# Four plain tiles instead of five in a gated channel mixer, and its block sums split 512 columns at a time

## The chip, the core and the metric

The kernel runs on one core of one Trainium2 chip. The metric is device time in microseconds (us): the median of several executions, beside one more execution that was profiled. A core has engines that work side by side, each through its own list of instructions in a fixed order: PE (TensorE, matmuls), DVE (VectorE), ACT (ScalarE), POOL (GpSimd), and SP, which here issues most DMAs. An engine's instruction waits until the instructions of other engines that it needs are done, and everything behind it on its engine waits with it.

## The reference

The reference is a two-layer trunk over 512 tokens of width 1024. Each layer has a token mixer (mLSTM in the first, banded attention in the second, with attention to a memory beside it) and then a channel mixer. The change is in the channel mixer alone:

```python
D_MODEL, SEQ = 1024, 512
D_FF = ((8 * D_MODEL // 3 + 127) // 128) * 128      # 2816

def causal_dwconv(x, w, b):
    k = w.shape[0]
    s = x.shape[1]
    xp = jnp.pad(x, ((0, 0), (k - 1, 0), (0, 0)))
    y = xp[:, 0:s] * w[0]
    for j in range(1, k):
        y = y + xp[:, j:j + s] * w[j]
    return y + b

def conv_ffn(h, w_up, conv_w, conv_b, w_down):
    u, g = jnp.split(h @ w_up, 2, axis=-1)
    g = causal_dwconv(g, conv_w, conv_b)
    return (jax.nn.silu(g) * u) @ w_down

# in each layer l
x = x + conv_ffn(rmsnorm(x, norm_ffn_g[l]), ffn_w_up[l], ffn_conv_w[l], ffn_conv_b[l], ffn_w_down[l])
```

## The kernel before

Everything is float32, and the kernel keeps its accuracy by splitting every operand of a matmul into a high part (`hi`, a cast on ACT, L140) and a low part (`lo`, the source minus `hi`, on DVE, L141). A product is then three matmuls: hi by hi, hi by lo, lo by hi (`mm3`, L194, L195, L196). Activations lie transposed, features on the 128 partitions and the 512 tokens along the columns. They are kept as pairs of tiles `u`.

The hidden width of a channel mixer is 2816, so it has 22 tiles of 128 hidden features, each with a gate and an up half. A tile is made in one of two ways.

- A **plain** tile (`plain`) multiplies gate and up in full: 8 blocks of the inner dimension, 512 columns, three matmuls each, for gate (into a `pmm` buffer of PSUM) and for up (`psc`). The weights of each half come by one DMA of 512 KB into a staging tile `wr`, of which there are three, and are split into `wh` and `wl`, of which there are three each. Behind the gate half come the three taps of the convolution (L692 on ACT, L685 twice on DVE), the silu (L722), the product with the up half (L727) and the split of the result (`keep`), which becomes `hid[j]`. The first three tiles also carry the factor of the norm (L718, L724).
- A **step** (`step`, from `later`) makes gate and up of one tile together with Winograd's form of Strassen's scheme: seven products of half the inner dimension and 256 columns, instead of eight. It needs sums of weight blocks (L888 on DVE, and their splits into `wh`, `wl`, `fh`, `fl`), and sums of activation blocks, which are made once per mixer.

The sums of activation blocks and the scaled activations come from the generator `forms`. It first yields eight times for the scaled tiles (L733) and their splits, then four times for the block sums: four subtractions of 256 columns (L751) and the splits of the results into parts, each time. `weave` takes a given share of a filler's yields per yield of a plain tile, so that `forms` runs between the blocks of plain tiles 1 to `PLAIN - 1`.

The down-projection is cut into 32 **units**, each 4 hidden tiles by 128 output features, 12 matmuls of 512 columns into one of two `ptr` buffers of PSUM (`down_products`). A unit's result is copied by ACT (L777) and added to DRAM by a DMA from POOL (L778). A pair of units shares one DMA of 512 KB and one split. `UNITS` says which units stand at which tile.

Two things set the order. Outside of `later` a scheduler orders each engine's list, so it may move instructions across the borders of the code's blocks. Inside `later` the lists of PE, ACT and DVE are written out by hand; the preparation of the first step stands ahead of that, and the scheduler may still place it between work of the last plain tile and its units.

Of the kernel before, what the change touches and what calls it, by code (L numbers as in the profile page):

```python
# [10 lines left out]
F32R = mybir.dt.float32r  # L11
# [5 lines left out]
P = 128  # L17
D = 1024
S = 512
# [20 lines left out]

PLAIN, UNSCALED, GROUP, LAST = 5, 3, 4, 6
UNITS = {PLAIN - 1: (0, 1, 2, 3), 5: (None, 4), 6: (None, 5), 7: (None, 6), 8: (None, 7)}
UNITS.update((j, (2 * j - 10, 2 * j - 9)) for j in range(9, 21))

H = S // 2
# [7 lines left out]
def trunk(  # L55
# [34 lines left out]
    def sb(tag, shape, dtype=F32):  # L90
        count[0] += 1
        return pool.tile(shape, dtype, tag=tag, name=f"{tag}{count[0]}", bufs=bufs[tag])

    def ps(tag):
        count[0] += 1
        return psum.tile([P, S], F32, tag=tag, name=f"p{tag}{count[0]}", bufs=pbufs[tag])
# [61 lines left out]
    turn = [0]  # L158
# [506 lines left out]
    class ChannelMixer:  # L665
# [64 lines left out]
        def forms(self):  # L730

            for j in range(KT):
                V.scalar_tensor_tensor(  # L733
                    xT[j], xT[j], self.gain[:, j : j + 1], self.norm.row, op0=ALU.mult, op1=ALU.mult
                )
                hi, lo = sb("u", [P, S], F32R), sb("u", [P, S], F32R)
                split(hi, lo, xT[j])
                self.ready.append((hi, lo))
                yield
            self.sums = []  # L740
            for k in range(KT // 2):
                b1, b2 = xT[k], xT[k + KT // 2]
                forms = []
                ta, tb = sb("t", [P, S]), sb("t", [P, S])
                for o, x, y in (
                    (ta[:, :H], b1[:, H:], b1[:, :H]),
                    (ta[:, H:], b2[:, H:], ta[:, :H]),
                    (tb[:, :H], b2[:, H:], b1[:, H:]),
                    (tb[:, H:], b2[:, :H], ta[:, H:]),
                ):  # L750
                    V.tensor_tensor(out=o, in0=x, in1=y, op=ALU.subtract)  # L751
                for t in (ta, tb):
                    for h in (t[:, :H], t[:, H:]):
                        both = sb("u", [P, S], F32R)
                        split(both[:, :H], both[:, H:], h)
                        forms.append(both)
                self.sums.append(forms)
                yield

# [3 lines left out]
            g, jj = divmod(q, KT // 2)  # L763
            return load(rows(ffn_w_down[self.l], 2 * jj * P, 2 * P, GROUP * g, GROUP * (g + 1)), GROUP, 2 * P)

        def down_products(self, u):
            g, j = divmod(u, KT)
            w = self.down[u // 2]
            o = ps("tr")
            c = slice(u % 2 * P, (u % 2 + 1) * P)  # L770
            for k in range(GROUP):
                mm3(o, w[0][:, k, c], w[1][:, k, c], *self.hid[GROUP * g + k], k == 0, k == GROUP - 1)
            return j, o

# [25 lines left out]

        def t(self, i):

            return [(p[i - 1][:, :H], p[i - 1][:, H:]) for p in self.sums]

        def later(self):

# [151 lines left out]
    def channel_mixer(l, act, norm, gain, beside):  # L958

        mixer = ChannelMixer(l, act, norm, gain, beside)  # L960
        forms = mixer.forms()
        run(mixer.plain(0))
        skips = -(turn[0] + 1) % 3
        for j in range(1, UNSCALED):
            turn[0] += j <= skips
            weave(mixer.plain(j), forms, KT / (16.0 * (UNSCALED - 1)))
# [2 lines left out]
        for j in range(UNSCALED, PLAIN):  # L969
            units = UNITS.get(j, ())  # L970
            raws = {u // 2: mixer.load_down(u // 2) for u in units[::2]}
            weave(mixer.plain(j), forms, 4 / (16.0 * (PLAIN - UNSCALED)))
            for u in units:
                if u // 2 not in mixer.down:
                    mixer.down[u // 2] = parts(raws[u // 2])
                mixer.add(*mixer.down_products(u))
        run(forms)
        mixer.later()
        reload_x()
# [303 lines left out]
    for j in range(KT):  # L1283
        wh, wl = weights(rows(ffn_w_down[0], j * P, P, FT - LAST, FT), LAST, P)
        o = ps("mm")
# [252 lines left out]
```

## Time and profile before

| | us |
|---|---|
| median of 3 executions | 1180.86 (1180.71 to 1181.27) |
| the profiled execution | 1181.04 |
| its span, first to last instruction | 1179.3 |
| PE busy | 1169.1 (99%) |
| DVE busy | 935.7 (79%) |
| ACT busy | 725.8 (62%) |
| POOL busy | 129.9 (11%) |

How the views are read: a row of the timeline is its start, its duration, engine, line, operation, output and input by the program's names, the size, and in brackets how long the engine was idle before and what ended that. Two matmuls that follow each other overlap, so the distance of their starts tells what one costs. Rows of the stretches give the stretch, then for each engine its busy time and number of instructions, the granted clock of PE, the DMA engines' busy share and GB/s. DMA rows give the size of a transfer and the median time from issue to landing.

The first mixer's plain tiles run from about 275 us of the span to 341, its steps to about 590; the second mixer's lie some 554 us later.

### The profile page before, as it was taken

Reading aid. Unit: us, or ns where it says so; the run is one execution under the profiler, and the core shown is the slowest. Engines: PE = TensorE matmul, PEld = TensorE weight load, DVE = VectorE, ACT = ScalarE, POOL = GpSimd, SP = SyncE. Lnnn points to the kernel's source line nnn. Section 1 sums busy time; section 2 is a strip of 40 time slices with the busy share of each in tenths; the row PEclk is TensorE's granted clock in tenths of the full one; section 3 lists DMA queues with packets and bytes.
Section 4 is the critical chain, followed back from the end, with each engine's and each line's share of the span. In section 5 each row is a group of like instructions: output and inputs, shape, how many; then the busy total and the mean of one; then the engine's idle time right before and its main releaser. Section 6 shows DMA issues by size and latency. Waiting matters only on the chain.

```text
span 1179.3 us, 18676 instructions
## 1 busy us (share of the span) xinstructions
PE 1169.1 (99%) x7007; PEld 1034.2 (88%) x7007; DVE 935.7 (79%) x1688; ACT 725.8 (62%) x1294; POOL 129.9 (11%) x222
## 2 busy tenths in 40 slices
PE   9999999999999999999999999999999999999997
PEld 9988888888889999999888888888889999999986
DVE  6877788887978877777698888897897877777755
ACT  6548677654655655555666667776565655555545
POOL 1111101000021111111020000101001011111100
PEclk9999999999999999999999999999999999999999
DMA  8645325244266677765564312335426466666551
GB/s 299 208 109 134 94 55 152 76 139 121 90 166 163 164 164 162 164 148 129 150 200 125 90 54 85 106 102 177 139 90 153 108 143 144 143 143 141 123 158 72
DMA packets 200156, 158.64 MB, mean 135 GB/s; under 512 B 8344, under 2 KB 179838, under 8 KB 200066
## 3 DMA queue, kind: packets, MB, share of 16 engines
q1 hardware_dynamic: 183906, 119.74, 34.6%
q0 software_dynamic: 15584, 36.67, 16.4%
q8 instruction: 55, 0.90, 0.3%
q10 hardware_dynamic: 576, 1.05, 0.2%
q14 instruction: 35, 0.29, 0.1%
HBM read 128.89 MB, written 32.46 MB: 137 GB/s over the span
## 4 chain that ended last, share of the span: by engine, by line
PE 94%; DVE 3%; ACT 1%; issue 0%; DMA 0%; SPq 0%; POOL 0%; ACTq 0%; POOLq 0%; DVEq 0%
PE pmm L194 18%; PE pmm L195 18%; PE pmm L196 18%; PE ptr L195 6%; PE ptr L194 6%; PE ptr L196 6%; PE psc L195 5%; PE psc L196 5%; PE psc L194 5%; PE psc L544 2%; PE ptr L1365 1%; PE ptr L1386 1%; PE ptr L1387 1%; PE ptr L627 1%; PE ptr L613 0%; DVE pt L141 0%
## 5 line engine op out<-in xcount | busy, mean ns | idle before, releaser
L194 PE MATMUL pmm<-u,wh 128*128 128x512 f32 (+1 forms) x968 | 333.2, 345 | 0.4 <-ACT u L140 0.2
L196 PE MATMUL pmm<-u,wl 128*128 128x512 f32 (+1 forms) x968 | 330.8, 342 | 0.0
L195 PE MATMUL pmm<-u,wh 128*128 128x512 f32 (+1 forms) x968 | 330.5, 342 | 0.0
L141 DVE TENSOR_TENSOR wl<-wr,wh 128x1024 fp32r<-128x1024 f32 (+3 forms) x172 | 199.6, 1162 | 101.8 <-ACT wh L140 101.4
L140 ACT CAST wh<-wr 128x1024 fp32r<-128x1024 f32 (+3 forms) x172 | 172.0, 1002 | 92.7 <-PE pmm L195 39.0
L196 PEld LDWEIGHTS pmm<-u,wl 128*128 128x128 f32 x968 | 181.9, 188 | 20.6
L194 PEld LDWEIGHTS pmm<-u,wh 128*128 128x128 f32 x968 | 181.8, 188 | 19.3 <-ACT u L140 1.1
L195 PEld LDWEIGHTS pmm<-u,wh 128*128 128x128 f32 x968 | 182.0, 188 | 18.5 <-DVE u L141 0.5
L194 PE MATMUL ptr<-u,wh 128*128 128x512 f32 x272 | 106.7, 392 | 0.0
L195 PE MATMUL ptr<-u,wh 128*128 128x512 f32 x272 | 106.5, 392 | 0.0
L196 PE MATMUL ptr<-u,wl 128*128 128x512 f32 x272 | 105.8, 389 | 0.0
L778 POOL DMA_DIRECT2D xspill<-t x64 | 55.6, 869 | 447.3 <-ACT t L777 437.5
L141 DVE TENSOR_TENSOR fl<-pt,fh 128x512 fp32r<-128x512 f32 x102 | 70.3, 689 | 11.2 <-ACT fh L140 8.5
L194 PE MATMUL pmm<-u,fh 128*128 128x256 f32 x272 | 75.4, 277 | 0.0
L195 PE MATMUL pmm<-u,fh 128*128 128x256 f32 x272 | 75.2, 276 | 0.0
L196 PE MATMUL pmm<-u,fl 128*128 128x256 f32 x272 | 75.2, 276 | 0.0
L195 PE MATMUL psc<-u,wh 128*128 128x256 f32 (+1 forms) x232 | 75.1, 324 | 0.0
L196 PE MATMUL psc<-u,wl 128*128 128x256 f32 (+1 forms) x232 | 75.1, 324 | 0.0
L194 PE MATMUL psc<-u,wh 128*128 128x256 f32 (+1 forms) x232 | 75.0, 324 | 0.0
L140 ACT CAST fh<-pt 128x512 fp32r<-128x512 f32 x102 | 62.7, 615 | 13.5 <-DVE pt L888 13.3
L950 ACT ACTIVATE t<-t 128x512 f32<-128x512 f32 x34 | 21.5, 632 | 79.2 <-DVE t L685 79.2
L777 ACT COPY t<-ptr 128x512 f32<-128x512 f32 x64 | 37.6, 587 | 51.6 <-PE ptr L196 51.6
(335 smaller groups left out, 2540.3 us busy)
## 6 DMA issues: line engine op xcount, KB each, us to landing
wr<-in_ffn_w_up_dram SPq DMA_DIRECT2D x54, 512.0 KB, 5.0
wr<-in_ffn_w_down_dram SPq DMA_DIRECT2D x38, 512.0 KB, 4.1
pt<-in_ffn_w_up_dram SPq DMA_DIRECT2D x34, 512.0 KB, 6.9
xspill<-t POOLq DMA_DIRECT2D x64, 256.0 KB, 4.7
wr<-in_a_w_in_dram SPq DMA_DIRECT2D x20, 512.0 KB, 3.8
wr<-in_w_kv_dram SPq DMA_DIRECT2D x12, 512.0 KB, 4.0
xspill<-fh POOLq DMA_DIRECT2D x16, 256.0 KB, 2.6
xspill<-fl POOLq DMA_DIRECT2D x16, 256.0 KB, 3.0
```

The lines of the kernel that those rows point to most:

```text
L140: high = A.copy(hi, src) if on_act else V.tensor_copy(hi, src)
L141: low = V.tensor_tensor(out=lo, in0=src, in1=f(hi), op=ALU.subtract)
L194: nc.tensor.matmul(o, lh, rh, start=first, stop=False, skip_group_check=more)
L195: nc.tensor.matmul(o, lh, rl, start=False, stop=False, skip_group_check=more)
L196: nc.tensor.matmul(o, ll, rh, start=False, stop=last, skip_group_check=more)
L544: nc.tensor.matmul(o, a, b, start=first and i == 0, stop=i == 1)
L627: nc.tensor.matmul(o2, vs[a][:, 2 * hp + h, :], p[h][:, a, :], start=i == 0, stop=i == 3)
L777: A.copy(t, o)
L778: G.dma_start(xspill[j], t, accum_op=ALU.add)
L950: A.activation(self.acc, self.acc, AF.Silu)
L1365: nc.tensor.transpose(tp[:, b * P : (b + 1) * P], es[T, h][:, b * P : (b + 1) * P], ident)
L1386: nc.tensor.matmul(o2[:, s * P :], w, hi_at(pts[h], s, s, TT - s), start=s == 0, stop=False)
```

## The change

`PLAIN` goes from 5 to 4: tile 4 becomes a step, so there are 18 steps instead of 17 in each mixer. Units 0, 1 and 2 stand behind the last plain tile, now tile 3, instead of units 0 to 3; unit 3 moves into the first step, tile 4. Since the units behind tile 3 need tile 3's own result, units 0 and 1 are started over their first three hidden tiles, and finished with the fourth (`k0`, `k1`, `o` of `down_products`). The four yields of the block sums now fall into one plain tile instead of two. Their parts are split as two pairs of 512 columns per pair of sums, instead of four of 256; the tiles `u` are as many as before. `skips` shifts by one which of the three weight buffers the tiles use. The number in brackets of `weave` changes with `PLAIN` by itself.

```diff
-PLAIN, UNSCALED, GROUP, LAST = 5, 3, 4, 6
-UNITS = {PLAIN - 1: (0, 1, 2, 3), 5: (None, 4), 6: (None, 5), 7: (None, 6), 8: (None, 7)}
+PLAIN, UNSCALED, GROUP, LAST = 4, 3, 4, 6
+UNITS = {PLAIN - 1: (0, 1, 2), 4: (None, 3), 5: (None, 4), 6: (None, 5), 7: (None, 6), 8: (None, 7)}
 UNITS.update((j, (2 * j - 10, 2 * j - 9)) for j in range(9, 21))
...
                 for t in (ta, tb):
-                    for h in (t[:, :H], t[:, H:]):
-                        both = sb("u", [P, S], F32R)
-                        split(both[:, :H], both[:, H:], h)
-                        forms.append(both)
+                    hi, lo = sb("u", [P, S], F32R), sb("u", [P, S], F32R)
+                    split(hi, lo, t)
+                    forms += [(hi[:, c], lo[:, c]) for c in (slice(0, H), slice(H, S))]
                 self.sums.append(forms)
                 yield
...
-        def down_products(self, u):
+        def down_products(self, u, k0=0, k1=GROUP, o=None):
             g, j = divmod(u, KT)
             w = self.down[u // 2]
-            o = ps("tr")
+            o = o or ps("tr")
             c = slice(u % 2 * P, (u % 2 + 1) * P)
-            for k in range(GROUP):
+            for k in range(k0, k1):
                 mm3(o, w[0][:, k, c], w[1][:, k, c], *self.hid[GROUP * g + k], k == 0, k == GROUP - 1)
             return j, o
...
         def t(self, i):
 
-            return [(p[i - 1][:, :H], p[i - 1][:, H:]) for p in self.sums]
+            return [p[i - 1] for p in self.sums]
...
         run(mixer.plain(0))
-        skips = -(turn[0] + 1) % 3
+        skips = -(turn[0] + 2) % 3
...
             weave(mixer.plain(j), forms, 4 / (16.0 * (PLAIN - UNSCALED)))
+            started = {}
             for u in units:
                 if u // 2 not in mixer.down:
                     mixer.down[u // 2] = parts(raws[u // 2])
-                mixer.add(*mixer.down_products(u))
+                if u < 2:
+                    started[u] = mixer.down_products(u, 0, GROUP - 1)[1]
+                if u == 1:
+                    for v, o in started.items():
+                        mixer.add(*mixer.down_products(v, GROUP - 1, GROUP, o))
+                if u >= 2:
+                    mixer.add(*mixer.down_products(u))
         run(forms)
         mixer.later()
```

The scheduler answers with another order at three places of each mixer; those of the first mixer are shown.

SP's list from tile 2's up weights on, before. `ffn_w_up` is gate, up or step weights, `ffn_w_down` the two loads for units 0 to 3.

```order
L153 DMA wr_3190<-in_ffn_w_up_dram 128x8x128
L153 DMA wr_3238<-in_ffn_w_up_dram 128x8x128
L153 DMA wr_3292<-in_ffn_w_up_dram 128x8x128
L153 DMA wr_3346<-in_ffn_w_down_dram 128x4x256
L153 DMA wr_3348<-in_ffn_w_down_dram 128x4x256
L153 DMA wr_3350<-in_ffn_w_up_dram 128x8x128
L153 DMA wr_3404<-in_ffn_w_up_dram 128x8x128
L153 DMA wr_3531<-in_ffn_w_up_dram 128x8x128
```

The same place now:

```order
L153 DMA wr_3190<-in_ffn_w_up_dram 128x8x128
L153 DMA wr_3238<-in_ffn_w_down_dram 128x4x256
L153 DMA wr_3240<-in_ffn_w_down_dram 128x4x256
L153 DMA wr_3242<-in_ffn_w_up_dram 128x8x128
L153 DMA wr_3306<-in_ffn_w_up_dram 128x8x128
L153 DMA wr_3427<-in_ffn_w_up_dram 128x8x128
```

The two down loads moved ahead of the last plain tile's gate (wr_3242) and up (wr_3306), which is tile 3 and no longer tile 4; behind those comes the first step's load (wr_3427).

DVE's list before, at the end of tile 3: its product with the up half (L727), the split of its result (u_3343), parts of a block sum, the split of the first down load (wl_3459) and that of tile 4's up weights (wl_3407).

```order
L727 TENSOR_TENSOR t_3287<-psc_3298,t_3287 128x512
L751 TENSOR_TENSOR t_3381<-fh_2364 128x256
L751 TENSOR_TENSOR t_3382<-fl_2372,fh_2364 128x256
L751 TENSOR_TENSOR t_3381<-fl_2372,t_3381 128x256
L141 TENSOR_TENSOR u_3343<-t_3287,u_3342 128x512
L751 TENSOR_TENSOR t_3382<-fl_2372,t_3381 128x256
L141 TENSOR_TENSOR u_3387<-t_3381,u_3387 128x256
L141 TENSOR_TENSOR u_3390<-t_3381,u_3390 128x256
L141 TENSOR_TENSOR u_3393<-t_3382,u_3393 128x256
L141 TENSOR_TENSOR u_3396<-t_3382,u_3396 128x256
L141 TENSOR_TENSOR wl_3459<-wr_3346,wh_3458 128x1024
L141 TENSOR_TENSOR wl_3407<-wr_3404,wh_3406 128x1024
```

DVE's list now, at the end of tile 3: wl_3407 is here the split of the second down load, wl_3430 that of the first step's weights, u_3367 that of tile 3's result.

```order
L727 TENSOR_TENSOR t_3301<-psc_3312,t_3301 128x512
L751 TENSOR_TENSOR t_3352<-fl_2374,t_3351 128x256
L141 TENSOR_TENSOR u_3358<-t_3351,u_3357 128x512
L141 TENSOR_TENSOR wl_3407<-wr_3240,wh_3406 128x1024
L141 TENSOR_TENSOR u_3362<-t_3352,u_3361 128x512
L141 TENSOR_TENSOR wl_3430<-wr_3427,wh_3429 128x1024
L141 TENSOR_TENSOR u_3367<-t_3301,u_3366 128x512
L887 TENSOR_TENSOR pt_3237<-pt_3237,wr_3427 128x512
L887 TENSOR_TENSOR pt_3237<-wr_3427,pt_3236 128x512
```

The split of tile 3's result moved behind the last parts of the block sums and behind the splits of the second down load and of the first step's weights; the first step's sums (L887) follow at once.

PE's list before, where units begin in earnest: the end of tile 4's up half (psc_3410) and unit 0 (ptr_3462), whose fourth hidden tile is u_3342 and u_3343.

```order
L195 MATMUL psc_3410<-u_3228,wh_3406 128x512
L196 MATMUL psc_3410<-u_3227,wl_3407 128x512
L196 MATMUL ptr_3462<-u_3137,wl_3459 128x512
L194 MATMUL ptr_3462<-u_3232,wh_3458 128x512
L195 MATMUL ptr_3462<-u_3233,wh_3458 128x512
L196 MATMUL ptr_3462<-u_3232,wl_3459 128x512
L194 MATMUL ptr_3462<-u_3342,wh_3458 128x512
L195 MATMUL ptr_3462<-u_3343,wh_3458 128x512
```

PE's list now, from the end of what units 0 (ptr_3374) and 1 (ptr_3384) do over three hidden tiles. u_3366 and u_3367 are tile 3's result, pmm_3463 is the first product of the first step.

```order
L196 MATMUL ptr_3384<-u_3232,wl_3371 128x512
L194 MATMUL pmm_3463<-u_3066,wh_3429 128x256
L195 MATMUL pmm_3463<-u_3067,wh_3429 128x256
L194 MATMUL ptr_3374<-u_3366,wh_3370 128x512
L194 MATMUL ptr_3384<-u_3366,wh_3370 128x512
L196 MATMUL pmm_3463<-u_3066,wl_3430 128x256
L194 MATMUL pmm_3463<-u_3083,wh_3429 128x256
L195 MATMUL pmm_3463<-u_3084,wh_3429 128x256
L196 MATMUL pmm_3463<-u_3083,wl_3430 128x256
L194 MATMUL pmm_3463<-u_3115,wh_3429 128x256
L195 MATMUL ptr_3374<-u_3367,wh_3370 128x512
L196 MATMUL ptr_3374<-u_3366,wl_3371 128x512
```

Units 0 and 1 are finished and the first step begun in turns, with the matmuls that need wl_3430 and u_3367 standing among those that do not; unit 2 follows behind. Outside of the channel mixers no list changes on PE, DVE and ACT, except for the names of the rows.

## The prediction, on record before the result

> **What bounds the kernel now.** I read the page first, for the busy shares and the chain that ended last.
>
> ```profile
> span 1179.3 us, 18676 instructions
> PE 1169.1 (99%) x7007; PEld 1034.2 (88%) x7007; DVE 935.7 (79%) x1688; ACT 725.8 (62%) x1294; POOL 129.9 (11%) x222
> ...
> PE 94%; DVE 3%; ACT 1%; issue 0%; DMA 0%; SPq 0%; POOL 0%; ACTq 0%; POOLq 0%; DVEq 0%
> ```
>
> TensorE (PE) works all the time and is 94% of the chain, so matmul time saved is time saved, as long as nothing else makes PE wait. VectorE (DVE) at 79% is an average; the view of stretches shows it around the places that change, the end of the plain tiles of both mixers.
>
> ```profile
> core 0: us, PE busy (x) PEld busy (x) DVE busy (x) ACT busy (x) POOL busy (x), PEclk, DMA share, GB/s
> 296.00:308.00 12.00, 12.00 (x55) 9.94 (x54) 12.00 (x19) 7.69 (x14) 0.00 (x0) 1.00 0.41 123
> 308.00:319.00 11.00, 11.00 (x50) 9.13 (x49) 11.00 (x23) 6.25 (x13) 0.00 (x0) 1.00 0.19 58
> 319.00:331.00 12.00, 12.00 (x55) 9.80 (x54) 12.00 (x26) 7.94 (x14) 0.00 (x0) 1.00 0.44 131
> 331.00:341.00 10.00, 10.00 (x46) 8.29 (x45) 7.35 (x11) 5.86 (x10) 2.60 (x3) 1.00 0.69 160
> 341.00:354.00 13.00, 13.00 (x105) 12.51 (x104) 8.56 (x12) 7.62 (x13) 3.51 (x5) 1.00 0.73 178
> 851.00:863.00 12.00, 12.00 (x55) 9.94 (x54) 12.00 (x19) 7.71 (x12) 0.00 (x0) 1.00 0.38 123
> ```
>
> The first four stretches are about plain tiles 2, 3 and 4 and then the four units of the first mixer, the fifth is the first step. DVE is busy in every microsecond of the three tiles, and has its first slack during the units; the second mixer has the same full stretch (the last row). So here two engines are full at once, and the change takes 11 us of PE work out of just this stretch.
>
> The timeline of PE gives the spacing of matmuls, which is what counts, since their durations overlap.
>
> ```profile
> 313.64 0.39 PE L194 MATMUL psc<-u,wh 128*128 128x512 f32 x1
> ...
> 319.08 0.39 PE L194 MATMUL pmm<-u,wh 128*128 128x512 f32 x1
> ...
> 340.68 0.39 PE L196 MATMUL ptr<-u,wl 128*128 128x512 f32 x1
> 340.90 0.28 PE L194 MATMUL pmm<-u,wh 128*128 128x256 f32 x1
> ...
> 462.75 0.28 PE L194 MATMUL pmm<-u,fh 128*128 128x256 f32 x1
> ...
> 467.52 0.28 PE L194 MATMUL pmm<-u,wh 128*128 128x256 f32 x1
> ```
>
> From 313.64 to 319.08 are the 24 matmuls of tile 3's up half: 0.2267 us each for 512 columns. From 462.75 to 467.52 are 42 of 256 columns: 0.1136 us each. The rows at 340.68 and 340.90 are the seam from the last unit to the first step: PE passes it without a gap.
>
> **The change part by part. PE.** Per mixer one plain tile goes, 2 x 8 x 3 = 48 matmuls of 512 columns, 48 x 0.2267 = 10.88 us. One step comes, 7 products x 4 x 3 = 84 matmuls of 256 columns, 84 x 0.1136 = 9.54 us. Units stay 32 in number. The saving is 1.34 us per mixer, 2.7 us in both, all of it on the path. The evictions confirm the step's length:
>
> ```profile
> 342.47 0.38 ACT L842 COPY t<-pmm 128x256 f32<-128x256 f32 x1
> 354.75 0.37 ACT L842 COPY t<-pmm 128x256 f32<-128x256 f32 x1 [0.61 <-PE pmm L196]
> ...
> 896.86 0.37 ACT L842 COPY t<-pmm 128x256 f32<-128x256 f32 x1
> ```
>
> One step with one unit took 12.28 us here; 9.54 + 12 x 0.2267 = 12.26.
>
> **DVE: where the cover goes.** The rows of DVE's timeline give its spacing and its slack.
>
> ```profile
> 275.27 0.69 DVE L658 TENSOR_TENSOR fl<-fl,pmm 128x512 f32<-128x512 f32 x1 [2.05 <-PE pmm L196]
> ...
> 298.08 0.74 DVE L733 SCALAR_TENSOR_TENSOR fl<-fl,cols,rb 128x512 f32<-128x512 f32 x1
> 298.74 1.22 DVE L141 TENSOR_TENSOR wl<-wr,wh 128x1024 fp32r<-128x1024 f32 x1
> 299.88 0.68 DVE L724 TENSOR_TENSOR t<-t,rb 128x512 f32<-128x512 f32 x1
> 300.48 0.68 DVE L141 TENSOR_TENSOR u<-fh,u 128x512 fp32r<-128x512 f32 x1
> ...
> 322.31 1.42 DVE L141 TENSOR_TENSOR u<-t,u 128x256 fp32r<-128x256 f32 x4
> 323.65 2.35 DVE L141 TENSOR_TENSOR wl<-wr,wh 128x1024 fp32r<-128x1024 f32 x2
> ...
> 331.71 0.69 DVE L727 TENSOR_TENSOR t<-psc,t 128x512 f32<-128x512 f32 x1
> ...
> 341.96 1.23 DVE L141 TENSOR_TENSOR wl<-wr,wh 128x1024 fp32r<-128x1024 f32 x1 [3.61 <-ACT wh L140]
> ```
>
> Start to start: 1.14 us for a split of 1024 columns, 0.60 for any two-tensor operation of 512, 0.66 for a scalar-tensor one, 0.335 for 256 columns. As a trial of these four numbers: between the starts of 299.88 and 331.71 the old order holds 6 splits, 16 of 512, 7 scalar-tensor and 32 of 256 columns: 6.84 + 9.6 + 4.62 + 10.72 = 31.8 us, against 31.83 in the rows. There is no idle time in it to lose, and 3.6 us of slack behind it.
>
> Now the new queue. The split of tile 2's gate weights moves up into the idle 2.05 us at 275, so the split that stood at 298.74 takes an earlier place, and L724 comes at 298.74 instead of 299.88. From its start to that of the split of step 4's first weights (wl_3430) the new order holds 4 splits, 16 operations of 256 columns, 5 scalar-tensor ones and 22 of 512: 4.56 + 5.36 + 3.3 + 13.2 = 26.4 us. In it the parts of the block sums cost 8 x 0.60 = 4.8 instead of 16 x 0.335 = 5.36: the wide form gives back 0.56 us.
>
> "VectorE: DVE Perf Modes" of the Trainium skill, section on the TRN2 errata, gives (N + 151) / 0.96 ns for an fp32 tensor_tensor: 691 ns at 512 and 424 at 256, as the 0.68 and 0.41 us in the rows. Taken as cost per instruction that makes the wide form worth 16 x 0.424 - 8 x 0.691 = 1.26 us, and the wait below 0.7 us shorter; the trace's spacing says that the fixed part overlaps, and it decides.
>
> One idle spot comes in. Staging has three buffers, and the two down-projection loads now hold two of them through tile 3. So gate 3, up 3 and step 4's weights go through the third, each load behind the split of the one before.
>
> ```profile
> 297.34 1.06 ACT L140 CAST wh<-wr 128x1024 fp32r<-128x1024 f32 x1 [0.80 <-ACT u L140]
> 298.30 0.63 ACT L722 ACTIVATE t<-t 128x512 f32<-128x512 f32 x1
> ...
> wr<-in_ffn_w_up_dram SPq DMA_DIRECT2D x7, 512.0 KB, 3.8
> ...
> wr<-in_ffn_w_up_dram SPq DMA_DIRECT2D x54, 512.0 KB, 5.0
> ```
>
> In the new queue gate 3's split starts five rows behind L724 (4 x 0.60 + 0.66 and L724's own 0.60), at 302.4, and is done at 303.6. Up 3 lands 3.8 us later (the stretch's median), at 307.4; ScalarE (ACT) casts it and a down load, 0.96 us each, and only then does the silu of tile 2 (0.63 us), which DVE's next L724 needs: 310.0, where DVE is ready at 309.9. I take 0.2 us. By the whole kernel's median of 5.0 us it would be 1.4 us, the upper end; 0 is the lower.
>
> So wl_3430 starts at 298.74 + 26.4 + 0.2 = 325.4 and is done 1.22 us later, at 326.6. Behind it stands u_3367, the low part of tile 3's result, done at 325.4 + 1.14 + 0.68 = 327.2.
>
> PE, as before, ends tile 3 at 319.08. It goes on with units 0 and 1 over three tiles (18 matmuls, 4.08), two matmuls of step 4 (0.23) and two on tile 3's high part (0.45): 323.84. The next matmul needs wl_3430. **PE waits 2.8 us**, about 1 us of it already two matmuls earlier, for ACT's cast of the high part (that cast needs DVE's L727, five rows of DVE ahead of wl_3430). Everything behind it on PE is queued, since an engine's order is fixed. Five matmuls on, at 327.2, u_3367 is just there. Unit 2 needs one of two PSUM buffers, so it waits for an eviction of unit 0, a copy of 0.59 us:
>
> ```profile
> 338.38 0.59 ACT L777 COPY t<-ptr 128x512 f32<-128x512 f32 x1 [0.89 <-PE ptr L196]
> ```
>
> That copy starts when unit 0's last matmul ends, 0.39 us after its start, while PE goes on for 0.9 us: 0.1 us more, and as much again for four releases between engines. I take 3.0 us per mixer. The ends: 4.2 with loads of 5.0 us; 2.0 if all of the 0.9 us that the moved split leaves idle at 275 (2.05 - 1.14) were filled as well.
>
> After it the rest is covered: DVE's seven remaining operations for step 4 (6 x 0.6 + 1.14 = 4.7 us) are done near 332, and PE needs the first of them behind unit 2 (2.7 us) and 15 short matmuls (1.7 us), near 332.9. The second mixer has the same order, and the same distances:
>
> ```profile
> 852.35 1.40 DVE L733 SCALAR_TENSOR_TENSOR fl<-fl,cols,rb 128x512 f32<-128x512 f32 x2
> 853.68 0.68 DVE L724 TENSOR_TENSOR t<-t,rb 128x512 f32<-128x512 f32 x1
> ```
>
> In the new order one L733 stands ahead of L724 instead of two, so it starts at 852.35 + 0.66 = 853.0. This mixer runs 554.39 us behind the first (evictions at 896.86 and 342.47): 853.0 - 554.39 = 298.6, within 0.15 us of the 298.74 there.
>
> At nothing I cost: the DMAs (two of 512 KB for a tile or a step, the same bytes), the additions to DRAM on GpSimd's queue (32 as before; it is 11% busy), and what a step asks of ACT and DVE while it runs: four evictions of 0.38 us on ACT, 7.62 of 13 us busy in the first step's stretch, and three sums of 256 columns on DVE, 8.56 of 13. Were that cover gone, they would cost 4 x 0.38 + 3 x 0.335 = 2.5 us.
>
> **Sum.** 2 x (3.0 - 1.34) = +3.3 us on the profiled execution, 1181.04 us (1.7 us more than its span): 1184.3. It lies 0.2 us above the median of 1180.86, so the median should be 1184.1. With the two ends of the wait: 2 x (2.0 - 1.34) = +1.3, 1182.2; 2 x (4.2 - 1.34) = +5.7, 1186.6.
>
> **The rivals.** *No wait*, only the saving: 1180.86 - 2.7 = 1178.2. It decides if wl_3430 is done by 323.8, for which DVE would have to be 2.8 us ahead in 26 us of queue without holes; the full stretches speak against it, and for it only that PE waits nowhere in the steps now. *Wait and saving cancel*, a wait of 0.2 to 2.5 us per mixer: 1178.6 to 1183.2, some 1181 at the wait of 1.34. For it speaks the idle time at 275; against it, that DVE's work between holds nothing that could start so early. *The staging chain sets the pace*: loads of 5.0 us in place of 3.8 set DVE back by 1.2 us per mixer, 1186.6 as above, and more if gate 3 is late too. Against it: the stretch's DMA share is 0.19 to 0.44, so a load is mostly alone. *A slower clock behind the wait*: if matmuls ran at twice their spacing for half of a step, 4.8 us per mixer, 1184.1 + 9.6 = 1193.7. No stretch of this trace shows a granted clock under 1.00, so I give it little.
>
> "TensorE: Matmul & The Clock Gate" of the Trainium skill, Part 1, has the clock halved after an idle window of about 3.4 us and released after as much work; two matmuls break up the wait here, so no window would be idle throughout. By its figure the estimate is 1.7 us per mixer, 1187.5.
>
> **How the numbers follow.** A change of 0.2%, 2.36 us, is about the least that a measurement of this kernel can tell from none. Chances: forecast 0.58 (a wait of 2.5 to 3.9 us; 1183.2 to 1186), no wait 0.11, cancelling 0.18, staging chain 0.09, clock 0.04. Slower: 0.58 + 0.09 + 0.04 = 0.71; same 0.18; faster 0.11. The range goes down into the cancelling case, to 1180.2, and up past the staging chain, to 1187.2; it leaves out the no-wait case, the clock and a little of the cancelling one.
>
> **What would show it.** Right: PE idle before L196 and L195 at the seam, released by DVE's splits, about 3 us in each mixer; the first step's eviction near 331.9 instead of 342.5; steps of 12.3 us as before; DVE full to about 327. Wrong: PE without a gap there, or a gap released by ACT or by a load, or a second gap in step 5.

## The result and the profile after

The changed kernel takes 1188.58 us (median of 6 runs, 1187.33 to 1191.31) where the kernel before takes 1181.07 (6 runs on the same chip): 1.0065 times as long, 95% interval 1.0055 to 1.0075. It is slower, as forecast, but by 7.5 us and not by 3.3; the time lies above the range. The profiled execution took 1187.92 us, 6.9 us more than the profiled one before; its span is 1186.1 us, 6.8 more.

The page of the changed kernel, its span, busy times and chain:

```profile
span 1186.1 us, 18831 instructions
PE 1170.8 (99%) x7079; PEld 1037.6 (87%) x7079; DVE 945.3 (80%) x1692; ACT 728.5 (61%) x1292; POOL 129.7 (11%) x222
...
PE 86%; DVE 10%; ACT 2%; DMA 1%; issue 1%; POOL 0%; ACTq 0%; DVEq 0%; POOLq 0%
```

DVE's part of the chain went from 3% to 10%, and PE's from 94% to 86%. The view of PE's waits names the places (engine, line, what was waited for: us in total, times, longest):

```profile
PE pmm L196 <- DVE wl L141: 3.1, 2, 1.6
PE ptr L194 <- ACT u L140: 1.5, 2, 0.9
...
PE psc L299 <- ACT t L140: 0.6, 1, 0.6
PE psc L299 <- DVE t L141: 0.2, 1, 0.2
```

The first two are the seam, once in each mixer. The last two are the norm of the first mixer, whose two matmuls stand within its first plain tile, a place to which the forecast gave no cost. To see what they cost I take every matmul's distance to the next and subtract 0.2267 us (512 columns) or 0.1136 (256): what is left is time that PE lost, whether the profile calls it idle or not. The rows of PE's timeline with such a loss, first mixer:

```profile
280.49 0.50 PE L299 MATMUL psc<-t,onesr 128*128 128x512 f32 x1 [0.63 <-ACT t L140]
281.22 0.51 PE L299 MATMUL psc<-t,onesr 128*128 128x512 f32 x1 [0.22 <-DVE t L141]
...
324.53 0.28 PE L195 MATMUL pmm<-u,wh 128*128 128x256 f32 x1
325.70 0.73 PE L194 MATMUL ptr<-u,wh 128*128 128x512 f32 x2 [0.90 <-ACT u L140]
328.00 0.58 PE L196 MATMUL pmm<-u,wl 128*128 128x256 f32 x1 [1.57 <-DVE wl L141]
...
329.24 0.63 PE L195 MATMUL ptr<-u,wh 128*128 128x512 f32 x1
329.67 0.63 PE L196 MATMUL ptr<-u,wl 128*128 128x512 f32 x1
...
331.62 0.40 PE L195 MATMUL ptr<-u,wh 128*128 128x512 f32 x1
331.85 0.39 PE L196 MATMUL ptr<-u,wl 128*128 128x512 f32 x1
```

Three losses stand here. At the norm 1.4 us (two waits, and the pipeline between them). At the seam 1.06 and 1.84, 2.9 us in all. And behind it the matmuls of 512 columns come 0.43 us apart (329.24 to 329.67) and not 0.23 (331.62 to 331.85): from 328.00 to 331.37 PE takes 3.37 us for work of 1.70, 1.7 us lost to a halved clock. In the second mixer the norm is not late and the clock stays full:

```profile
839.06 0.63 PE L299 MATMUL psc<-t,onesr 128*128 128x512 f32 x2
...
883.42 0.73 PE L194 MATMUL ptr<-u,wh 128*128 128x512 f32 x2 [0.63 <-ACT u L140]
885.73 0.38 PE L196 MATMUL pmm<-u,wl 128*128 128x256 f32 x1 [1.57 <-DVE wl L141]
```

Its seam loses 0.80 + 1.86, and 0.4 more around the start of unit 2: 3.1 us. Another 0.3 us goes in the second step of each mixer (ahead of the matmuls at 351.02 and 907.54), where the kernel before loses none. Sum: 1.4 + 2.9 + 1.7 + 3.1 + 0.6 less the 2.7 us saved is +7.0, against 6.9 in the profiled executions.

The norm's delay is on the other engines' timelines. Before, the norm's last square (L288) and its sum on DVE (L289) come as soon as their input is there:

```profile
275.99 0.63 ACT L288 ACTIVATE t<-fl 128x512 f32<-128x512 f32 x1 [4.15 <-DVE fl L658]
...
276.66 0.69 DVE L289 TENSOR_TENSOR rb<-rb,t 128x512 f32<-128x512 f32 x1 [0.70 <-ACT t L288]
```

Now ACT's cast and DVE's split of tile 2's gate weights stand ahead of them:

```profile
276.88 1.05 ACT L140 CAST wh<-wr 128x1024 fp32r<-128x1024 f32 x1 [5.16 <-DMA wr<-in_ffn_w_up_dram]
277.83 0.62 ACT L288 ACTIVATE t<-fl 128x512 f32<-128x512 f32 x1
...
277.96 1.23 DVE L141 TENSOR_TENSOR wl<-wr,wh 128x1024 fp32r<-128x1024 f32 x1 [2.12 <-ACT wh L140]
279.10 0.69 DVE L289 TENSOR_TENSOR rb<-rb,t 128x512 f32<-128x512 f32 x1
```

The cast waits for its load until 276.88, and the square (L288), whose input had been ready since about 276, waits behind it; DVE's sum comes at 279.10 and no longer at 276.66. DVE's idle time at 275 could hold the split, but ACT's queue could not hold the cast. The trace of before could have told: there the load in this place of SP's list, issued at 271.99, took 5.1 us to land, until 277.1.

### The profile page after: what moved, and what is told of

Read it like the earlier page. It is cut to its first block, busy times and chain, and to the rows that moved or that the text cites. A ratio compares the mean times of both kernels' runs of the same rounds, so it can differ in the third digit from the quotient of the medians.

```text
span 1186.1 us, 18831 instructions
## 1 busy us (share of the span) xinstructions
PE 1170.8 (99%) x7079; PEld 1037.6 (87%) x7079; DVE 945.3 (80%) x1692; ACT 728.5 (61%) x1292; POOL 129.7 (11%) x222
## 4 chain that ended last, share of the span: by engine, by line
PE 86%; DVE 10%; ACT 2%; DMA 1%; issue 1%; POOL 0%; ACTq 0%; DVEq 0%; POOLq 0%
PE pmm L194 17%; PE pmm L196 17%; PE pmm L195 17%; PE ptr L195 6%; PE ptr L196 6%; PE ptr L194 6%; PE psc L195 4%; PE psc L196 4%; PE psc L194 4%; PE psc L544 2%; DVE u L141 2%; DVE wl L141 2%; DVE t L685 1%; PE ptr L1371 1%; ACT wh L140 1%; DMA wr<-in_ffn_w_up_dram 1%
## 5 line engine op out<-in xcount | busy, mean ns | idle before, releaser
L140 ACT CAST wh<-wr 128x1024 fp32r<-128x1024 f32 (+3 forms) x170 | 169.6, 1001 | 88.5 <-PE pmm L195 39.0
L141 DVE TENSOR_TENSOR fl<-pt,fh 128x512 fp32r<-128x512 f32 x108 | 74.2, 689 | 11.6 <-ACT fh L140 8.8
L194 PE MATMUL pmm<-u,fh 128*128 128x256 f32 x288 | 79.8, 277 | 0.0
L195 PE MATMUL pmm<-u,fh 128*128 128x256 f32 x288 | 79.6, 276 | 0.0
L196 PE MATMUL pmm<-u,fl 128*128 128x256 f32 x288 | 79.6, 276 | 0.0
L140 ACT CAST fh<-pt 128x512 fp32r<-128x512 f32 x108 | 66.5, 617 | 12.3 <-DVE pt L887 12.1
L195 PE MATMUL psc<-u,wh 128*128 128x256 f32 (+1 forms) x224 | 71.1, 317 | 0.0
L196 PE MATMUL psc<-u,wl 128*128 128x256 f32 (+1 forms) x224 | 71.0, 317 | 0.0
L194 PE MATMUL psc<-u,wh 128*128 128x256 f32 (+1 forms) x224 | 71.0, 318 | 0.0
```

The costliest lines, as they stand in the source:

```text
L140: high = A.copy(hi, src) if on_act else V.tensor_copy(hi, src)
L141: low = V.tensor_tensor(out=lo, in0=src, in1=f(hi), op=ALU.subtract)
L194: nc.tensor.matmul(o, lh, rh, start=first, stop=False, skip_group_check=more)
L195: nc.tensor.matmul(o, lh, rl, start=False, stop=False, skip_group_check=more)
L196: nc.tensor.matmul(o, ll, rh, start=False, stop=last, skip_group_check=more)
```

## The experiments

All numbers of PE's lost time are read as above, from one profile of each kernel. Times of a run are medians, beside runs of the kernel before on the same chip (1180.85 to 1180.96 us). "The changed kernel" is the 1188.58 us of the result; e10 measured it again, at 1187.92.

**e1: the cast and the split go behind the norm's.** The edit queues both behind ACT's cast of the norm's sum of squares; in the compiled program no other row of any engine moves, and only the first mixer is touched. (Its added lines shift the later line numbers, by 7 from the norm's matmuls on; the code is shortened.)

```diff
 split(*parts, self.acc)
+self.cast = <ACT's instruction of this split>
...
-wh, wl = weights(rows(w, c0, P), n, P)
+raw = load(rows(w, c0, P), n, P)
+with tc.issue_after(after):        # tile 2's gate only
+    wh, wl = parts(raw)
```

> The changed kernel with one thing moved: in mixer 0 the cast and the split of tile 2's gate weights are queued behind the norm's own cast on ACT, instead of ahead of its last square. No other row moves on any engine. Theory (the cast waits for its load and holds the norm up): the two L299 matmuls come without a wait, the 1.4 us lost there in mixer 0 come back, DVE's queue starts 1.3 us earlier too, and the seam's wait stays at about 2.9 us: 1188.6 - 1.4 = 1187.2 us. Rival (DVE sets the pace from the norm to the seam, so what PE gets back at the norm it loses at the seam): L299 without a wait, the seam's wait 1.4 us longer, 1188.6 us.

Measured: 1187.67 us, ratio 1.0055 (1.0042 to 1.0069). By the time alone theory and rival can't be told apart; by the profile they can. PE's timeline, both mixers:

```profile
279.84 0.63 PE L306 MATMUL psc<-t,onesr 128*128 128x512 f32 x2
...
324.70 0.74 PE L194 MATMUL ptr<-u,wh 128*128 128x512 f32 x2 [1.13 <-ACT u L140]
327.01 0.38 PE L196 MATMUL pmm<-u,wl 128*128 128x256 f32 x1 [1.57 <-DVE wl L141]
...
881.40 0.73 PE L194 MATMUL ptr<-u,wh 128*128 128x512 f32 x2 [0.82 <-ACT u L140]
883.71 0.38 PE L196 MATMUL pmm<-u,wl 128*128 128x256 f32 x1 [1.57 <-DVE wl L141]
```

The norm's pair comes at 279.84 without a wait, as in the kernel before (279.83). At the first seam PE loses 1.30 + 1.86 us instead of 1.06 + 1.84, so 0.3 of the 1.4 us is given back there. The theory holds in the main: the norm's wait is the cast's. The half clock, though, is now in the second mixer and not in the first, so the profile's span is nearly the old one (1185.9 us).

**e2: idle matmuls in the wait.** Unit 0's first three blocks run once more, into a spare PSUM tile that nothing reads.

```diff
+if u == 0:
+    spare = ps("tr")
+    for k in range(GROUP - 1):
+        w = mixer.down[0]
+        mm3(spare, w[0][:, k, :P], w[1][:, k, :P], *mixer.hid[k], k == 0, k == GROUP - 2)
 if u < 2:
     started[u] = mixer.down_products(u, 0, GROUP - 1)[1]
```

> The changed kernel with nine idle matmuls (unit 0's first three blocks once more, into a spare PSUM tile, 2.04 us) on PE right ahead of the seam, in both mixers; ACT and DVE have the same rows. If PE truly waits there, these cost nothing: the seam's gap shrinks from 2.9 to 0.9 us in mixer 0 and from 3.3 to 1.3 in mixer 1, and L196 still starts as DVE's split ends. Theory of the clock (the gaps of about 1.1 and 1.9 us halve the clock behind them in mixer 0): no half clock behind the shorter gap, so 1188.6 - 1.7 = 1186.9 us. Rival (the half clock has another cause): double spacing from 328 on as before, 1188.6 us. If PE did not wait there: 1188.6 + 4.1 = 1192.7 us.

Measured: 1188.69 us, ratio 1.0064 (1.0051 to 1.0076). At the seams of this kernel:

```profile
327.35 0.39 PE L196 MATMUL pmm<-u,wl 128*128 128x256 f32 x1 [0.97 <-DVE wl L141]
...
885.38 0.39 PE L196 MATMUL pmm<-u,wl 128*128 128x256 f32 x1 [1.32 <-DVE wl L141]
```

PE truly waits there: with 2.04 us more work it comes to the first mixer's matmul at 327.35, not later than the 328.00 of the changed kernel. The clock stays full behind both seams, and the mean granted clock of the five runs is 0.998 or 0.999, where the changed kernel's six have 0.994 to 0.998. So much speaks for the theory of the clock. The time does not show the gain, and the expected 1186.9 us is a miss. PE's lost time says where it went: 1.7 us less for the clock and 0.7 less at the norm, but the seams did not take up all of the idle matmuls. With these in them they took 3.7 us in the first mixer, 0.7 more than in the changed kernel, and 4.6 in the second, 1.5 more. There the split came late because gate 3's load did (5.3 us to land instead of 3.8, DVE idle for 1.41 us ahead of 859.24, where the changed kernel has none). Why the first seam grew stays open.

**e3: the low parts of the block sums on GpSimd.**

```diff
-split(hi, lo, t)
+A.copy(hi, t)
+G.tensor_tensor(out=lo, in0=t, in1=f(hi), op=ALU.subtract)
```

> The changed kernel with the low parts of the block sums (8 subtractions of 512 columns per mixer) on GpSimd instead of DVE: 8 x 0.60 = 4.8 us off DVE's queue between the norm and the seam. Theory (DVE's queue makes the seam's wait): both waits go, and the half clock with them: 1188.6 - 2.9 - 1.7 - 3.3 = 1180.7 us, with the norm's stall of mixer 0 still in it. Rival (GpSimd is too slow for eight of them in some 20 us, and the first step waits for its parts): a gap a few matmuls behind the old seam, released by POOL, 1182 to 1190 us. Rival (the staging chain sets the pace): waits as before, released by a load or by ACT, 1188.6 us.

Measured: 1201.5 us, ratio 1.0171 (1.0157 to 1.0185). None of the three expectations had this. GpSimd's timeline at one of the subtractions:

```profile
324.34 1.41 POOL L755 TENSOR_TENSOR u<-t,u 128x512 fp32r<-128x512 f32 x1 [1.01 <-ACT u L754]
```

And DVE's around it:

```profile
322.10 0.74 DVE L685 SCALAR_TENSOR_TENSOR t<-pmm,cols,t 128x511 f32<-128x511 f32 x1
324.19 0.41 DVE L751 TENSOR_TENSOR t<-fl,fh 128x256 f32<-128x256 f32 x1
324.52 1.51 DVE L751 TENSOR_TENSOR t<-fl,t 128x256 f32<-128x256 f32 x1
```

DVE's subtraction of 256 columns, 0.41 us at 324.19, takes 1.51 at 324.52, while GpSimd works on its own of 1.41 us. The operation at 322.10, one of whose inputs is in PSUM, keeps its 0.74 us beside GpSimd's four (316.60 to 323.33). The low parts taken from DVE come back as time in which it stands still, and one costs 1.4 us or more instead of 0.60. At each seam PE waits some 5 us for the high part of tile 3's result, which needs DVE's L727. "SBUF — State Buffer" of the Trainium skill, in the sections on the two separate sides and on who interferes with whom, says that DVE and GpSimd share a pair of ports by an exclusive lock: a DVE operation with two SBUF inputs contends with a GpSimd operation that reads SBUF, and one with at most one SBUF input does not. These rows agree.

**e4: the old split of the sums' parts, 256 columns at a time, in the changed kernel.** The edit puts back the loop over halves, as the change's diff shows it.

> The changed kernel with the block sums' parts split 256 columns at a time, as before: in both mixers 16 subtractions of 256 columns for 8 of 512. By the spacing of DVE's rows (0.335 and 0.60 us) the seam's wait grows by 0.56 us per mixer, 1189.7 us; the page VectorE: DVE Perf Modes of the Trainium skill (TRN2 errata) gives, taken as cost per instruction, 1.26 us per mixer, 1191.1 us. In both, the longer gap may halve the clock in mixer 1 as well, 1.7 us more. Should the wide form be worth nothing: 1188.6 us.

Measured: 1194.6 us, ratio 1.0111 (1.0098 to 1.0125). No expectation is met, because the order moves too: unit 0's and unit 1's low weights are split behind the block sums, and units 0 and 1 wait for them.

```profile
326.24 0.80 PE L196 MATMUL ptr<-u,wl 128*128 128x512 f32 x1 [3.65 <-DVE wl L141]
```

DVE's own price can still be read: from L718 of tile 0 to the first step's sums (L887, L888 here) DVE takes 43.19 us in this kernel and 42.40 in the changed one, with 0.51 and 0.24 us of idle time at tile 2's L724: 0.5 us more work for 16 narrow subtractions instead of 8 wide ones. The spacing of rows gave 0.56. "VectorE: DVE Perf Modes" of the Trainium skill, section on the TRN2 errata, taken as cost per instruction, gave an estimate of 1.26. The trace decides for the spacing. The wide form is worth much more than this to the changed kernel, 6 us, but by the order that comes with it.

**e5: half of the block sums' parts into the first step.** On top of e1, the casts and low parts of the second sum of each pair are made in the first step, ahead of its s3 product (the code is shortened).

```diff
-for t in (ta, tb):
-    hi, lo = sb("u", [P, S], F32R), sb("u", [P, S], F32R)
-    split(hi, lo, t)
+<ta's split here, tb's put in self.late>
...
 then(nxt, "sums")
+for finish in self.late:
+    finish()
 then(tail, "gated")
```

> The changed kernel with the cast held behind the norm's (as in e1) and, in both mixers, the parts of the second block sum of each pair (4 casts, 4 subtractions of 512 columns) moved out of tile 3 into the first step, ahead of its third sum. DVE has 4 x 0.60 = 2.4 us less ahead of the seam, and the order puts the low part of tile 3's result and unit 2 ahead of the matmuls on step 4's low weights. Theory (DVE's queue alone makes the wait, and the wait the half clock): PE waits 0.4 to 0.5 us at the seam, none or up to 1.5 us in the first step ahead of its s3 product, no half clock: saving 2.7, so 1180.9 - 2.7 + 2 x (0.5 to 1.9) = 1179 to 1182 us, on the good side of the kernel before or level with it. Rival (the wait only moves into the first step, where DVE is 2.4 us later): 1183 to 1187 us, the gap released by DVE behind the seam.

Measured: 1183.85 us, ratio 1.0024 (1.0013 to 1.0035), 4.7 us less than the changed kernel, and in the rival's range. The seams lose 0.8 and 0.4 us, no window behind them runs at half clock, and 1.2 to 1.3 us per mixer are lost ahead of s3, a little before each of its four blocks:

```profile
333.75 0.28 PE L194 MATMUL pmm<-u,wh 128*128 128x256 f32 x1
334.19 0.38 PE L195 MATMUL pmm<-u,wh 128*128 128x256 f32 x1 [0.16 <-DVE u L141]
```

So with less in DVE's queue the seam's wait shrinks, and part of the work taken out is late in its new place too.

**e6: no low parts.** As in e3, but the subtractions are left out.

```diff
-split(hi, lo, t)
+A.copy(hi, t)
+lo = hi
```

> The changed kernel without the subtractions for the low parts of the block sums: the high part stands in for the low one in the step's products, so this part of the result is left out (8 subtractions of 512 columns per mixer, 4.8 us of DVE). ACT's casts, PE's matmuls and the loads are all there. Theory (DVE's queue makes the seam's wait): no wait at the seam and no half clock; the norm's 1.4 us in mixer 0 stay: 1180.9 - 2.7 + 1.4 = 1179.6 us. Rival (the staging chain or ACT's casts set the pace): a wait of 1 us or more stays in each mixer, released by ACT or a load, 1182 to 1186 us.

Measured: 1180.91 us, ratio 0.9997 (0.9988 to 1.0006); the profiled execution took 1180.08. The one wait of PE in the mixers that is left:

```profile
PE psc L299 <- ACT t L140: 0.7, 1, 0.7
```

Nothing is left of the seams' waits and of the half clock. The norm's loss (1.5 us) stays, and some 0.35 us each at the start of unit 2 in the first mixer and in the second step of both; ahead of the first mixer this execution lost 0.8 us less than that of the kernel before. 1181.04 - 2.7 + 1.5 + 1.0 - 0.8 is 1180.0. With 4.8 us less on DVE per mixer and as many casts and loads as before, 7.7 us are back. So DVE's queue sets the seam, and neither the staging chain nor ACT does, with one reserve: the scheduler's order around the seam moved with the edit, and PE's first matmuls of the first step no longer stand ahead of the finish of units 0 and 1. The split that the seam waits for starts at 321.66 there and not at 326.73, so in the old order too it would have been done before PE needs it.

**e7: the wide split alone, with five plain tiles.** The edit is that part of the change's diff.

> The kernel before with the wide split alone (8 subtractions and casts of 512 columns per mixer for 16 of 256), still five plain tiles. By the spacing of DVE's rows 0.56 us per mixer less on DVE, where PE waits for nothing: 1180.9 us, no change. Rival (the chain of before holds some DVE time in this stretch on the path): up to 1.1 us faster, 1179.8 us.

Measured: 1181.08 us, ratio 1.0001 (0.9992 to 1.001). As expected, nothing: PE does not wait there, so DVE's 0.5 us is hidden.

**e8: four staging buffers.**

```diff
-"u": (50, S), ... "wr": (3, D)
+"u": (48, S), ... "wr": (4, D)
```

> The changed kernel with four staging buffers for loads instead of three (two buffers fewer for split parts), so gate 3's load need not wait for the split before it. This reorders other places of the kernel too, so the reading is that of the trace at the seam. Theory (DVE's own queue, 26 us without holes, makes the wait): DVE's idle time between the norm and the seam goes from 0.3 us to 0, the seam's wait stays at 2.6 to 3.1 us. Rival (the chain of load, cast and split through one buffer sets the pace): the wait falls by 1 us or more in both mixers.

Measured: 1192.26 us, ratio 1.0093 (1.0079 to 1.0107). Other places of the kernel got longer, so only the seam is read:

```profile
328.09 0.39 PE L196 MATMUL pmm<-u,wl 128*128 128x256 f32 x1 [2.09 <-DVE wl L141]
...
890.14 0.39 PE L196 MATMUL pmm<-u,wl 128*128 128x256 f32 x1 [2.08 <-DVE wl L141]
```

DVE has no idle time of 0.1 us from 286 to 328, and PE still loses 0.20 + 2.37 us at the first seam. Its norm comes without a wait, so the nearer comparison is e1, whose first seam lost 3.2 us: the one buffer costs some tenths, up to 0.6 us, and not the wait.

**e9 and e12: the same work at two other places of the first step.** As e5, with the four late casts and subtractions at the head of the step (e9), and behind ACT's copy of its first product (e12).

```diff
 w.split_fourth()
+for finish in self.late: finish()          # e9
 ...
 A.copy(new.up[:, :H], r1[:, :H])
+for finish in self.late: finish()          # e12
```

> As e5, with the four late casts and subtractions queued at the head of the first step, where DVE stood idle for 1.3 us in e5, instead of behind its second sum. Theory (DVE's queue): the waits ahead of the s3 product (about 1.3 us per mixer in e5) go, those at the seam (0.8 and 0.4 us) stay: 1183.85 - 2.6 = 1181.3 us, level with the kernel before. Rival (the casts stand ahead of ACT's eviction of the first product, so PE waits there instead): 1183 to 1185 us, with a gap released by ACT before the s2 product.

> As e9, with the four late casts and subtractions queued behind ACT's copy of the first product instead of ahead of it. Theory (in e9 PE waited 0.76 us per mixer ahead of the s2 product because that copy stood behind the four casts): this gap goes, those at the seam (0.9 and 0.7 us, on the low part of tile 3's result and on unit 0's eviction) stay, no half clock: 1182.6 - 1.5 = 1181.1 us, within 0.1% of the kernel before. Rival (the DVE work moved into the step is late in any place): a gap ahead of s3, released by DVE, 1182 to 1184 us.

Measured: e9 1182.62 us, ratio 1.0019 (1.001 to 1.0028); e12 1180.89, ratio 0.9994 (0.9985 to 1.0003). In e9 the s3 product waits for nothing, but the s2 product does, as the rival had it, for ACT's copy of r1, which stands behind the four casts:

```profile
PE pmm L194 <- ACT t L857: 0.9, 2, 0.5
```

In e12 this line is gone from the waits, and only a remainder of the seam is left (1.3 us of lost time in the first mixer, 0.68 of it idle, and 0.3 in the second). The expected 1181.1 us is met. e12 is 7.7 us under the changed kernel and level with the kernel before; it does not beat it.

**e10 and e11: the changed kernel once more, and e1 with e2's idle matmuls.**

> The changed kernel, unaltered, on the chip of these runs: a second profile of it. If the half clock behind the seam depends on where the gap falls and not on the order of the program, it may show in another mixer, or in both or none, with the time moving by 1.7 us for each; the gaps themselves, 1.1 and 1.9 us, and the norm's wait of 1.4 us stay where the order puts them: 1188.6 us.

> The changed kernel with the cast held behind the norm's (e1) and the nine idle matmuls ahead of the seam (e2). Theory: the norm's 1.4 us and the half clock both go; the seam's wait of about 3.2 us holds the 2.04 us of idle matmuls: span 1179.3 - 2.7 + 2 x 3.2 = 1183.0, 1184.7 us, plus up to 1.4 us per mixer where gate 3's load lands late, as it did in e2. Rival (the clock or the idle matmuls have another price that e2's time hides): 1187 us or more.

Measured: e10 1187.92 us, ratio 1.0062 (1.0048 to 1.0076), with gaps, norm wait and half clock all where they were; e11 1187.87, ratio 1.0056 (1.0041 to 1.0072). e11 missed its expectation by 3 us. Its trace has no norm wait and no half clock, and seams of 4.0 and 4.1 us with the idle matmuls and the start of unit 2 in them, so the span should have been 1179.3 - 2.7 + 8.1 = 1184.7; it was 1186.7. Of these 2 us 1.4 lie ahead of the first mixer (its norm's pair at 281.23 instead of 279.84; the waits show 1.6 us at the kernel's start, for ACT's `cols`), and the rest in the steps behind the seams, some 0.35 us in each mixer, as in the changed kernel. Such waits at the start come and go with the execution (0.5 us for another load there in the kernel before, 1.6 in e12), so a mechanism of 1 or 2 us has to be read in the trace and not in the medians.

## Why the prediction was wrong

**The saving, right.** First steps' evictions lie 12.33 us apart, as forecast, though the first comes at 334.85 and not near 331.9; the norm's 1.4 us and the clock's 1.7 account for the difference:

```profile
334.85 0.38 ACT L841 COPY t<-pmm 128x256 f32<-128x256 f32 x1
...
347.18 0.37 ACT L841 COPY t<-pmm 128x256 f32<-128x256 f32 x1
```

**The wait at the seam, right.** Forecast: 3.0 us per mixer, 2.8 for wl_3430, about 1 us of it two matmuls earlier for ACT's cast, and 0.1 for unit 2's buffer. Measured: 2.9 and 3.1, in those pieces, with 0.4 instead of 0.1 around unit 2 where it can be read (second mixer). The count of DVE's queue holds as well: from L724 to wl_3430's split it gave 26.7 us (298.74 to 325.4), and the trace has 26.9 (299.84 to 326.73); e6 shows that the queue sets it, e4 that the wide form saves 0.5 and not 1.26 us, and the idle time for the staging chain, taken at 0.2 us, is 0.24 in the first mixer.

**The hoisted split, wrong: this is the step that failed first.** The forecast looked at DVE alone ("moves up into the idle 2.05 us at 275") and gave it no cost. The split brings its cast along, the cast waits for a load, and ACT runs its queue in order; so the norm came 1.4 us later in the first mixer, for PE and for DVE alike, while the seam kept its wait. None of the rows that it shows of before is ACT's at that place. e1 takes it away.

**The clock, wrong: the rival with a chance of 0.04 is what happened.** It was set aside because no stretch of the trace before showed a granted clock under 1.00, and with "two matmuls break up the wait here, so no window would be idle throughout". The first does not hold for that trace's end: from 1172.57 to 1175.98 PE has nothing to do, and from 1175.98 on the clock is 0.50. The second is what failed. The measured loss is 1.7 us, in one mixer of the two; the forecast's price for this rival, 4.8 us per mixer, was too high. The 1.7 us per mixer of its estimate from "TensorE: Matmul & The Clock Gate" of the Trainium skill, Part 1, is the size that the one loss had. The stretches of PE's timeline, cut to 3.41 us, show what decides. Columns: busy time of PE (and number of matmuls), of PEld (its weight loads), DVE, ACT, POOL, then the granted clock; the first three rows and the next two are the changed kernel's first and second seam:

```profile
324.55:327.96 3.41, 0.99 (x5) 0.35 (x3) 3.41 (x5) 1.10 (x2) 0.00 (x0) 1.00 0.09 25
327.96:331.37 3.41, 3.37 (x11) 2.98 (x12) 2.40 (x4) 0.72 (x2) 0.10 (x1) 0.50 0.37 129
331.37:334.78 3.41, 3.41 (x19) 2.93 (x19) 2.15 (x3) 3.37 (x6) 1.70 (x2) 1.00 1.01 209
880.92:884.33 3.41, 2.60 (x12) 1.69 (x10) 3.41 (x7) 1.76 (x3) 0.00 (x0) 1.00 0.00 0
884.33:887.74 3.41, 2.01 (x11) 1.65 (x11) 3.41 (x6) 0.59 (x2) 0.00 (x0) 1.00 0.47 154
1181.28:1184.69 3.41, 0.00 (x0) 0.00 (x0) 0.72 (x1) 0.69 (x1) 0.00 (x0) 0.50 0.40 154
```

The last row is the kernel's end, where PE has stopped: its half clock begins 853.3 us, 250 times 3.413, after that of the first seam. So the windows are on a fixed grid, and the rows of the second seam are cut on the same grid. "TensorE: Matmul & The Clock Gate" of the Trainium skill, Part 1, has a free-running window of 3413 ns, which this agrees with; its "idle window" is narrower than what the rows show, since a window with 0.99 us of matmuls in it halved the clock of the next. The same cut in e1, first the two windows of its first seam and the next, then the one of its second and the next:

```profile
321.45:324.86 3.41, 2.28 (x12) 1.76 (x11) 3.41 (x7) 1.76 (x3) 0.00 (x0) 1.00 0.00 0
324.86:328.28 3.42, 1.85 (x10) 1.32 (x11) 3.42 (x6) 0.00 (x0) 0.00 (x0) 1.00 0.49 153
328.28:331.69 3.41, 3.39 (x17) 2.65 (x16) 2.46 (x4) 3.25 (x6) 1.79 (x2) 1.00 0.19 50
881.23:884.64 3.41, 1.67 (x8) 1.20 (x9) 3.41 (x5) 0.12 (x1) 0.00 (x0) 1.00 0.44 139
884.64:888.05 3.41, 3.41 (x11) 2.73 (x9) 2.11 (x4) 2.43 (x4) 1.77 (x2) 0.50 0.23 65
```

In these windows PE busy for 0.99 and 1.67 us was followed by half clock, and 1.85, 2.01, 2.28 and 2.60 by full. But busy time alone does not draw the line, for in e8, far from the seams, a window with less than e1's 1.67 us kept the clock:

```profile
796.88:800.29 3.41, 1.59 (x8) 0.91 (x6) 2.90 (x7) 1.83 (x4) 0.00 (x0) 1.00 0.09 27
800.29:803.71 3.42, 3.42 (x17) 2.78 (x17) 2.95 (x15) 2.59 (x12) 0.00 (x0) 1.00 0.45 131
```

The durations in the rows overlap. Counted by their spacing (0.2267 us for 512 columns, 0.1136 for 256), the matmuls of this window are 1.39 us of work and those of e1's are 1.25, and so counted (other sizes in proportion to their columns) the two sides do not mix in any of the 14 traces behind the kernel's first 12 us: up to 1.25 us the clock halves, from 1.39 on it stays full. The same two gaps fall into one window or into two, as the grid happens to lie, and so the clock halves behind one seam and not the other; this also fits runs of one program that differ by 1 to 4 us with mean clocks from 0.994 to 0.998. That the spread of the runs is this and nothing else is argued, not shown.

**The steps behind the seam, a small miss.** "After it the rest is covered" put them at nothing, and a second gap in step 5 was named as a sign of being wrong. It is there, 0.3 us in each mixer. Its cause stays open.

**The sum.** Forecast for the profiled execution: +3.3 us. With 1.4 for the norm, 1.7 for the clock, 0.6 for the two later steps, and the seams at 2.9 and 3.1 instead of 3.0 each, it is +7.0, against 6.9. Without the norm's and the clock's 3.1 us the median of 1188.58 would have been 1185.5, within the range. Of the other rivals, the staging chain adds up to 1.4 us where a load is late in one execution (e2), but it does not make the wait (e8). *No wait* comes about only where DVE has less to do (e6).

## What to carry to other kernels

When a change moves one operation into another engine's idle time, follow its whole chain, with the cast and the load that it brings, through the queue of each engine in it: one entry that waits for a transfer holds up all that stand behind it. Where two engines are both full, a few us taken from one only show how late the other is; the cure here was to move work of the second (e12), and its place within the step was worth 3 us (e5 against e12). A wait on PE of 2 to 3 us can cost half as much again behind it, if a window of the clock holds most of it.

## What was not expected of the hardware

The clock halves behind a window of 3.41 us that is far from idle: with 1.25 us of matmul work in it, by spacing, the next window ran at half clock, with 1.39 us at full. At half clock, a window with 2.57 us busy did not bring it back (e4's first seam: two windows in a row at half, and full clock behind them):

```profile
325.40:328.81 3.41, 2.57 (x6) 2.08 (x7) 3.41 (x4) 0.31 (x1) 0.00 (x0) 0.50 0.40 106
328.81:332.22 3.41, 3.41 (x9) 2.64 (x9) 3.41 (x7) 1.76 (x3) 0.00 (x0) 0.50 0.70 207
```

Eight subtractions of 512 columns on GpSimd cost more than they free on DVE, since the two engines hold each other up: 1.41 us on GpSimd made DVE's 0.41 us into 1.51.
